# Four projections of a retention branch, each cut into seven block products, with tokens on the partitions

## The chip, the cores and the metric

One core of one Trainium2 chip runs the whole kernel. The metric is the device time of one execution in microseconds (us). The kernel before takes 1122.37 us, the median of three runs that lie between 1118.46 and 1122.79 us. The five engines are named as in the profile: PE (matrix products), DVE (element by element), ACT (scale, copy and functions), POOL and SP (here used almost only to issue DMA transfers). Each engine works through its own queue in order; an instruction that waits holds back everything behind it on that engine.

## What is computed

A decoder layer of width 1024 on 512 tokens. A retention branch with four heads and a latent attention branch read the same normalised input; each is projected to width 1024 and gated; their sum goes through `w_o`, and an MLP and a per-layer embedding follow. The change is in the third line here and the first product of the fourth:

```
ro = retention(q, k, v)                       # 512 tokens x 4 heads x 512
ro = rms_norm(ro, ret_norm)                   # per head: a factor per token, a gain per channel
a_ret = (ro * silu(rg)) @ w_br                # the branch: (512 x 2048) @ (2048 x 1024)
mixed = sigmoid(gr) * a_ret + sigmoid(gm) * a_mla
x = x + mixed @ w_o
```

Per head the branch is a product of 512 tokens x 512 channels with a 512 x 1024 part of `w_br`, and the four heads are summed.

## The kernel before

**Products.** Everything is float32 in accuracy, made from float32r products: each operand is split into a high part and a low remainder, and `mm3` issues three matmuls (low by high, high by low, high by high), the low part of its stationary operand first. A weight chunk of 512 KB arrives as a 128 x 1024 buffer `wr_...`; ACT copies its high part to `wh_...` (L261) and DVE subtracts to get `wl_...` (L265, or L267 with a sign). Activations are split in the same way by `split` (ACT L306, DVE L307).

**Steps.** The program is a list of steps, each with the key of its weight chunk. `run_steps` goes through it: the split of a chunk is put one step ahead of the step that uses it, its transfer three steps ahead; there are three split buffers and six raw ones. PE's order is that of the list. The other engines follow the order in which the scheduler placed their instructions.

**Block products.** Some projections (`rv`, `rg`, `up`/`dn`) are done as a set of seven block products (numbered 1 to 7) in place of eight: some of their weights are a sum of two blocks, and this sum is made in the transfer. For product 7 POOL issues a second transfer that adds a block onto the buffer already loaded by SP, for 5 another; the weights of 6 and 4 are added onto the buffer of 7 after its previous value was split. So 5 transfers on SP and 4 adding ones on POOL serve one chunk set.

**A retention head.** Steps `rq` (2), `rk` (2), for heads 0 and 2 fourteen steps `rv` that serve two heads, seven steps `rg` with scores (`rs`), the weighted sum (`ro`) and the statistics between them. DVE reads `rq` and `rk` out of PSUM for the rotation (L774, L775: two products per block; L780, L781: the combination) and splits them. The gated output `og` has channels on partitions.

**The branch of a head** runs during the next head: `ret_factor` multiplies `og` by the factor per token, which PE first spreads over the partitions (`pbo`, four small transposes), and splits it to `rog`; `branch_r` then is four steps of 24 matmuls, with the weights stationary and 512 tokens on the free dimension, each giving two of the eight 128-channel blocks of the sum. ACT copies a result out (`rt`), and POOL adds it onto a buffer in memory, one of eight per head (head 0 writes). For heads 1 and 3 the four branch steps follow `rk`; for head 2 they stand between the first `rv` steps. Behind head 3 the sum comes back (`re`), the last head's branch adds its result from PSUM with DVE (L867), `mix` applies the two gates' results (L897, L898) and splits for `wo`.

## Time and profile before

| | us |
|---|---|
| median of three runs | 1122.37 |
| the profiled execution | 1125.78 |
| its span | 1124.0 |
| PE busy, share of the span | 1107.5, 99% |
| DVE busy, share | 734.9, 65% |
| ACT busy, share | 536.7, 48% |
| head 1 begins (first `rq` matmul) | 374.7 |
| head 2 begins | 451.4 |
| head 3 begins | 570.7 |
| tail begins (`gr` step 5) | 647.4 |
| the run of `wo` products begins | 689.2 |
| first `up` product | 730.3 |

The profiled execution is 3.4 us above the median of the runs, and 1.8 us of it lie outside the span. The granted clock of PE was 0.997 of full speed on average. The page of a profile gives sums per engine, the chain of work that ended last, and the costliest groups; a timeline gives one engine's instructions with the idle time before each and what ended it.

### The profile page before, as it was taken

Reading aid. Unit: us, or ns where it says so; the run is one execution under the profiler, and the core shown is the slowest. Engines: PE = TensorE matmul, PEld = TensorE weight load, DVE = VectorE, ACT = ScalarE, POOL = GpSimd, SP = SyncE. Lnnn points to the kernel's source line nnn. Section 1 sums busy time; section 2 is a strip of 40 time slices with the busy share of each in tenths; the row PEclk is TensorE's granted clock in tenths of the full one; section 3 lists DMA queues with packets and bytes.
Section 4 is the critical chain, followed back from the end, with each engine's and each line's share of the span. In section 5 each row is a group of like instructions: output and inputs, shape, how many; then the busy total and the mean of one; then the engine's idle time right before and its main releaser. Section 6 shows DMA issues by size and latency. Waiting matters only on the chain.

```text
span 1124.0 us, 14722 instructions
## 1 busy us (share of the span) xinstructions
PE 1107.5 (99%) x5549; PEld 939.0 (84%) x5549; DVE 734.9 (65%) x1206; ACT 536.7 (48%) x762; POOL 85.4 (8%) x113
## 2 busy tenths in 40 slices
...
GB/s 264 59 98 106 67 99 57 128 210 211 190 225 173 87 212 121 135 202 253 137 92 220 223 172 154 196 274 117 171 165 168 176 166 155 186 123 219 146 29 75
DMA packets 59223, 175.97 MB, mean 157 GB/s; under 512 B 7248, under 2 KB 8656, under 8 KB 58896
## 3 DMA queue, kind: packets, MB, share of 16 engines
q1 hardware_dynamic: 45168, 129.66, 33.8%
q0 software_dynamic: 13840, 45.36, 20.9%
...
q10 hardware_dynamic: 144, 0.03, 0.0%
...
## 4 chain that ended last, share of the span: by engine, by line
PE 87%; DVE 4%; DMA 4%; ACT 2%; issue 2%; SPq 0%; ACTq 0%; DVEq 0%; POOLq 0%
PE up L168 16%; PE dn L168 14%; PE br L168 6%; PE rg L168 5%; PE rv L168 5%; PE pg L168 4%; PE gr L168 4%; PE rq L168 4%; PE rk L168 4%; PE bm L168 4%; PE wo L168 4%; DMA wr_rg<-wstream 4%; PE gm L168 3%; PE ro L168 3%; PE sc L168 2%
## 5 line engine op out<-in xcount | busy, mean ns | idle before, releaser
L168 PE MATMUL dn<-wh_dn,cl 128*128 128x512 f32 x224 | 87.2, 389 | 0.0
L168 PE MATMUL dn<-wh_dn,ch 128*128 128x512 f32 x224 | 87.2, 389 | 0.0
L168 PE MATMUL dn<-wl_dn,ch 128*128 128x512 f32 x224 | 87.1, 389 | 0.0
L261 ACT ACTIVATE wh_dn<-wr_dn 128x1024 fp32r<-128x1024 f32 x32 | 34.0, 1062 | 75.5 <-PE up L168 54.3
L261 ACT ACTIVATE wh_up<-wr_up 128x1024 fp32r<-128x1024 f32 x32 | 33.9, 1061 | 57.4 <-PE up L168 29.3
L265 DVE TENSOR_TENSOR wl_dn<-wr_dn,wh_dn 128x1024 fp32r<-128x1024 f32 x32 | 39.0, 1220 | 27.5 <-ACT wh_dn L261 27.5
L265 DVE TENSOR_TENSOR wl_rg<-wr_rg,wh_rg 128x1024 fp32r<-128x1024 f32 x20 | 24.3, 1223 | 40.7 <-ACT wh_rg L261 40.4
L265 DVE TENSOR_TENSOR wl_up<-wr_up,wh_up 128x1024 fp32r<-128x1024 f32 x32 | 39.1, 1222 | 17.4 <-ACT wh_up L261 17.4
L970 DVE SCALAR_TENSOR_TENSOR f<-up,bcx 128x512 f32<-128x512 f32 x32 | 20.6, 685 | 44.1 <-PE up L168 44.1
L168 PEld LDWEIGHTS dn<-wl_dn,ch 128*128 128x128 f32 x224 | 42.0, 188 | 8.8
L168 PEld LDWEIGHTS dn<-wh_dn,cl 128*128 128x128 f32 x224 | 42.0, 188 | 8.7
L168 PEld LDWEIGHTS dn<-wh_dn,ch 128*128 128x128 f32 x224 | 42.0, 188 | 8.6
L261 ACT ACTIVATE wh_dn<-dr_dn 128x1024 fp32r<-128x1024 f32 x24 | 25.5, 1060 | 42.2 <-PE up L168 29.1
L223 POOL DMA_DIRECT2D dr_dn<-wstream x24 | 21.4, 892 | 306.3 <-DMA dr_dn<-wstream 182.0
L265 DVE TENSOR_TENSOR wl_dn<-dr_dn,wh_dn 128x1024 fp32r<-128x1024 f32 x24 | 29.3, 1222 | 22.4 <-ACT wh_dn L261 22.4
L261 ACT ACTIVATE wh_rv<-wr_rv 128x1024 fp32r<-128x1024 f32 x28 | 29.6, 1058 | 28.7 <-PE rv L168 11.8
L261 ACT ACTIVATE wh_rg<-wr_rg 128x1024 fp32r<-128x1024 f32 x28 | 29.3, 1054 | 28.9 <-DMA wr_rg<-wstream 23.6
L265 DVE TENSOR_TENSOR wl_br<-wr_br,wh_br 128x1024 fp32r<-128x1024 f32 x16 | 19.5, 1219 | 21.6 <-ACT wh_br L261 21.6
L1028 DVE TENSOR_TENSOR d<-d,dn 128x1024 f32<-128x1024 f32 x24 | 29.2, 1219 | 6.5 <-PE dn L168 6.5
L265 DVE TENSOR_TENSOR wl_rv<-wr_rv,wh_rv 128x1024 fp32r<-128x1024 f32 x20 | 24.4, 1223 | 13.6 <-ACT wh_rv L261 13.6
L861 ACT ACTIVATE rt<-br 128x512 f32<-128x512 f32 x24 | 14.3, 596 | 36.1 <-PE br L168 30.9
L644 ACT ACTIVATE p<-p,ng,hr 128x128 f32<-128x128 f32 (+3 forms) x32 | 20.6, 646 | 15.6 <-DVE ng L642 15.5
...
## 6 DMA issues: line engine op xcount, KB each, us to landing
...
```

Of the source, the lines that this page charges most:

```text
L168: return tc.keep_in_program_order(nc.tensor.matmul(*a, **k))
L223: nc.gpsimd.dma_start(raw, chunk(("w", blk, kb, fb, c)), accum_op=ALU.add)
L261: i = ACT(hi, raw, AF.Copy, scale=sign)
L265: TT(lo, raw, hi.bitcast(F32), op=ALU.subtract)
L644: ACT(cols[b], cols[b], AF.Exp, bias=ng[:, b:b + 1], scale=d["rq"][:, b], accum_out=sums[:, b:b + 1])
L861: ACT(t, ps, AF.Copy)
L970: STT(u[:, i], ps[:, i], 0.0, V["bcx2"], op0=ALU.max, op1=ALU.mult)
L1028: TT(to, to, dps[p], op=ALU.add if sign > 0 else ALU.subtract)
```

## The change

The branch of each head becomes a set of seven block products, each 12 matmuls. Its stationary operand is now the gated output (256 channels by 256 tokens, two blocks of 128 channels), its moving one a 256 x 512 weight block held as 128 x 1024, so tokens lie on the partitions of the result. The operands are blocks of `og` or a sum or difference of two, kept in `bs` and `bt`, and split to `bx` (head, product, h or l). The factor of a token is now a scalar per partition: ACT applies it (with its sign, `ro` or `nro`) when it reads the result (`rt`), or DVE for the last head. Two results per product are added onto memory, fourteen per head. `ret_factor`, `pbo` and `rog` are gone. The steps are laid between the next head's `rq` and `rk`. In the tail the sum comes back with tokens on partitions, DVE adds the last head's fourteen results, 32 transposes on PE (`ret_turn`) turn it, and `mix` reads PSUM. The weights come as for the other block products.

```diff
--- before.py
+++ after.py
@@ -52,7 +52,7 @@
 
 C_ID, C_MASK, C_IND, C_INVR, C_INVM, C_SGN, C_N = 0, 128, 256, 260, 261, 262, 263
 
-NDYN, NKEEP, NW, NRAW, NDRAW, AHEAD, PREP, EARLY, PAD = 45, 16, 3, 6, 4, 1, 3, 5, 104
+NDYN, NKEEP, NW, NRAW, NDRAW, AHEAD, PREP, EARLY, PAD = 47, 16, 3, 6, 4, 1, 3, 5, 72
 GROUPS = DFF // 1024
 
 
@@ -105,8 +105,6 @@
         for key, o in (("rq", O_RQ), ("rk", O_RK)):
             for n in range(2):
                 add((key, h, n), "w_in", full, _rng(o + h * RQK + n * P, P))
-        for k in range(4):
-            add(("br", h, k), "w_br", _rng(h * RV, RV), _rng(2 * k * P, 2 * P))
 
     for kb in range(2):
         for fb in range(2):
@@ -114,6 +112,7 @@
                 for c in range(2):
                     add(("w", ("rv", q), kb, fb, c), "w_in", _rng(kb * S + c * 2 * P, 2 * P), _rng(O_RV + (2 * q + fb) * RV, RV))
             for h in range(RH):
+                add(("w", ("br", h), kb, fb, 0), "w_br", _rng(h * RV + kb * 256, 256), _rng(fb * S, S))
                 add(("w", ("rg", h), kb, fb, 0), "w_in", _rng(kb * S, S), _rng(O_RG + h * RV + fb * 256, 256))
     for gg in range(GROUPS):
         for n in range(8):
...
@@ -797,14 +796,14 @@
 
     def ret_attend(h):
         d = R[h]
+        d["o"] = [dyn.tile([P, 2, S], F32, tag="o2", name=f"og{h}{k}", bufs=2) for k in range(2)]
         for m in range(4):
             ps = B(f"ro{h}{m}")
             for j in range(4):
                 N = max(256, (4 - j) * P)
                 mm3(ps[:, S - N:S], cut(d["v"][j], m * P), at(j), j == 0, j == 3)
-            t, sq = T(f"og{h}{m}"), T(f"sqo{h}{m}")
-            ACT(t, ps, AF.Copy, scale=g(G_RET + 4 * h + m))
-            d["og"].append(t)
+            sq = T(f"sqo{h}{m}")
+            ACT(d["o"][m // 2][:, m % 2], ps, AF.Copy, scale=g(G_RET + 4 * h + m))
             ACT(sq, ps, AF.Square)
             if m:
                 TT(d["sq"], d["sq"], sq, op=ALU.add)
...
@@ -837,40 +838,83 @@
                 d["z"][12] = T(f"z{h}_12")
             TT(d["z"][blk], z, sg, op=ALU.mult)
 
+    def two(t):
+        return t.rearrange("p (k c) -> p k c", k=2)
+
     def ret_gated(h):
         d = R[h]
-        for m in range(4):
+        for k in range(2):
             for r in range(2):
-                cs, z = slice(r * 256, r * 256 + 256), d["z"][10 * (r + 1) + 1 + m // 2]
-                TT(d["og"][m][:, cs], d["og"][m][:, cs], z[:, m % 2 * 256:m % 2 * 256 + 256], op=ALU.mult)
-
-    def ret_factor(h):
-        d, r = R[h], R[h]["r"]
-        bc = bcast(B(f"pbo{h}"), lambda b: r[:, b:b + 1])
-        for m in range(4):
-            TT(d["og"][m], d["og"][m], bc, op=ALU.mult)
-            new = K if m < 2 and h < RH - 1 else T
-            d["rog"][m] = split(d["og"][m], None, hi=new(f"rog{h}{m}h", F32R), lo=new(f"rog{h}{m}l", F32R))
-
-    def branch_r(w, h, half):
+                o = d["o"][k][:, :, r * 256:r * 256 + 256]
+                TT(o, o, two(d["z"][10 * (r + 1) + 1 + k]), op=ALU.mult)
+
+    def branch_operand(h, p):
+
+        (a, b), lo_, hi_ = R[h]["o"], slice(0, 256), slice(256, 512)
+        if p == 7:
+            R[h]["s"] = T(f"bs{h}")
+        sv = two(R[h]["s"]) if "s" in R[h] else None
+        if p in (1, 2, 4):
+            src = (a if p == 1 else b)[:, :, hi_ if p == 4 else lo_]
+        elif p == 5:
+            src = two(T(f"bt{h}"))
+            TT(src, a[:, :, hi_], b[:, :, hi_], op=ALU.subtract)
+        else:
+            src = sv
+            if p == 7:
+                TT(sv, a[:, :, hi_], a[:, :, lo_], op=ALU.subtract)
+            else:
+                TT(sv, b[:, :, hi_ if p == 6 else lo_], sv, op=ALU.subtract)
+        hi, lo = two(T(f"bx{h}{p}h", F32R)), two(T(f"bx{h}{p}l", F32R))
+        split(src, None, hi=hi, lo=lo)
+        R[h]["x", p] = [(hi[:, k], lo[:, k]) for k in range(2)]
+
+    brps = {}
+
+    def branch_r(w, h, p):
+
+        ch, d = CHAIN[p], R[h]
+        if p in (1, 7, 2):
+            brps[ch] = [B(f"br{h}{p}{i}") for i in range(2)]
+        for k in range(2):
+            for i in range(2):
+                mm3(brps[ch][i], cut(d["x", p][k], i * P), cut(w, k * S, S), p in (1, 7, 2) and k == 0, k == 1,
+                    skip_group_check=True)
+        to, f = {1: (11, "nr"), 7: (22, "r"), 6: (21, "nr"), 2: (11, "r"), 5: (22, "r"), 4: (21, "nr"), 3: (12, "r")}[p]
         for i in range(2):
-            n = 2 * half + i
-            ps = proj(B(f"br{h}{n}"), R[h]["rog"], w, i * P, 2 * P)
-            if h < RH - 1:
-                t = T(f"rt{h}{n}")
-                ACT(t, ps, AF.Copy)
-                if h == 0:
-                    ret[n] = aside(f"ret{n}", t)
-                else:
-                    nc.gpsimd.dma_start(ret[n], t, accum_op=ALU.add)
+            b, n = 2 * (to // 10 - 1) + i, to % 10 - 1
+            r, ps = d[f][:, b:b + 1], brps[ch][i]
+            if h == RH - 1:
+                STT(ret[b, n], ps, r, ret[b, n], op0=ALU.mult, op1=ALU.add)
+                continue
+            t = T(f"rt{h}{p}{i}")
+            ACT(t, ps, AF.Copy, scale=r)
+            if h == 0 and p in (1, 7, 6, 3):
+                ret[b, n] = aside(f"ret{b}{n}", t)
             else:
-                TT(ret[n], ret[n], ps, op=ALU.add)
+                nc.gpsimd.dma_start(ret[b, n], t, accum_op=ALU.add)
+
+    def ret_back():
+        for b in range(4):
+            for n in range(2):
+                t = K(f"re{b}{n}")
+                nc.sync.dma_start(t, ret[b, n])
+                ret[b, n] = t
+
+    trp = {}
+
+    def ret_turn(n):
+
+        trp[n] = B(f"tr{n}")
+        for b in range(4):
+            MM(trp[n][:, b * P:b * P + P], ret[b, n // 4][:, n % 4 * P:n % 4 * P + P], ident, is_transpose=True,
+               start=b == 0, stop=b == 3, skip_group_check=True)
 
...
     def mix(n):
         if n < EARLY:
             ACT(sgr[n], sgr[n], AF.Sigmoid)
-        TT(ret[n], ret[n], sgr[n], op=ALU.mult)
-        TT(ret[n], ret[n], zm[n], op=ALU.add)
-        mixed[n] = split(ret[n], f"mix{n}")
+        TT(sgr[n], trp[n], sgr[n], op=ALU.mult)
+        TT(sgr[n], sgr[n], zm[n], op=ALU.add)
+        mixed[n] = split(sgr[n], f"mix{n}")
 
 
...
+    def branch_steps(h, seq):
+
+        order = [p for p in seq if not callable(p)]
+        step(None, branch_operand, h, order[0])
+        for p in seq:
+            if callable(p):
+                p()
+                continue
+            if order.index(p) < 6:
+                step(None, branch_operand, h, order[order.index(p) + 1])
+            step(("sw", ("br", h), p, 0), branch_r, h, p)
+
     for h in range(RH):
-        for key in ("rq", "rk"):
-            for n in range(2):
-                step((key, h, n), ret_qk, h, key, n)
-                if h and (key, n) == ("rq", 0):
-                    step(None, ret_factor, h - 1)
-        left = [(("br", h - 1, k), branch_r, h - 1, k) for k in range(4 if h else 0)]
+        def qk(key, n, h=h):
+            return lambda: step((key, h, n), ret_qk, h, key, n)
+
+        qk("rq", 0)()
+        if h:
+            branch_steps(h - 1, [1, qk("rq", 1), 7, 2, qk("rk", 0), 6, 5, qk("rk", 1), 4, 3])
+        else:
+            for key, n in (("rq", 1), ("rk", 0), ("rk", 1)):
+                qk(key, n)()
         for p in (1, 7, 2, 6, 5, 4, 3) if h % 2 == 0 else ():
             for c in range(2):
                 step(("sw", ("rv", h // 2), p, c), ret_v, h // 2, p, c)
             if h == 0 and p in (1, 7, 2):
                 step(None, x_operand, {1: 6, 7: 5, 2: 3}[p])
-            if left:
-                step(*left.pop(0))
-        for st in left:
-            step(*st)
         for p in (1, 7):
             step(("sw", ("rg", h), p, 0), ret_gate, h, p)
         step(None, ret_scores, h)
@@ -1219,17 +1274,19 @@
         for p in (4, 3):
             step(("sw", ("rg", h), p, 0), ret_gate, h, p)
         step(None, ret_gated, h)
+    step(None, ret_back)
     for n in range(8):
         step(None, reload, n)
-    for n in range(EARLY, 8):
-        step(("gr", n), gate_r, n)
-        if n == EARLY:
-            step(None, ret_factor, RH - 1)
-    for k in range(4):
-        step(("br", RH - 1, k), branch_r, RH - 1, k)
-        step(None, mix, 2 * k)
-        step(None, mix, 2 * k + 1)
-    for n in range(2):
+    step(("gr", 5), gate_r, 5)
+    branch_steps(RH - 1, [1, 7, 2, lambda: step(("gr", 6), gate_r, 6), 6, 5, 4, 3])
+    for n in range(4):
+        step(None, ret_turn, n)
+        step(None, mix, n)
+    step(("gr", 7), gate_r, 7)
+    for n in range(4, 8):
+        step(None, ret_turn, n)
+        step(None, mix, n)
+    for n in range(3):
         step(("o", n), out_part, n, 0)
     for n in range(8):
         step(("o", n), out_proj, n)
```

The order of the instructions, as built, at three places. In the names, `br070` is head 0, product 7, chunk 0; `bx01` is head 0, product 1; the last number tells a buffer apart. Line numbers of the kernel after are its own.

DVE, from the first reads of head 1's `rq` (L774, L775). Before:

```order
L774 TENSOR_TENSOR rqa10_3906<-rq10_3881,trc_952 128x512
L775 TENSOR_TENSOR rqb10_3907<-rq10_3881,trs_953 128x512
L851 TENSOR_TENSOR og00_3691<-og00_3691,pbo0_3910 128x512
L851 TENSOR_TENSOR og01_3708<-og01_3708,pbo0_3910 128x512
L851 TENSOR_TENSOR og02_3726<-og02_3726,pbo0_3910 128x512
L307 TENSOR_TENSOR rog00l_3917<-og00_3691,rog00h_3916 128x512
L851 TENSOR_TENSOR og03_3744<-og03_3744,pbo0_3910 128x512
L307 TENSOR_TENSOR rog01l_3922<-og01_3708,rog01h_3921 128x512
L307 TENSOR_TENSOR rog02l_3927<-og02_3726,rog02h_3926 128x512
L265 TENSOR_TENSOR wl_rk_1_1_3983<-wr_rk_1_1_3980,wh_rk_1_1_3982 128x1024
L307 TENSOR_TENSOR rog03l_3932<-og03_3744,rog03h_3931 128x512
```

And now (L773, L774 are the same reads):

```order
L773 TENSOR_TENSOR rqa10_3902<-rq10_3877,trc_952 128x512
L774 TENSOR_TENSOR rqb10_3903<-rq10_3877,trs_953 128x512
L264 TENSOR_TENSOR wl_br070_3950<-wr_br070_3922,wh_br070_3949 128x1024
L306 TENSOR_TENSOR bx01l_3907<-og00_3678,bx01h_3906 128x512
L865 TENSOR_TENSOR bs0_3910<-og00_3678 128x512
L306 TENSOR_TENSOR bx07l_3913<-bs0_3910,bx07h_3912 128x512
L867 TENSOR_TENSOR bs0_3910<-og01_3679,bs0_3910 128x512
L264 TENSOR_TENSOR wl_br020_3997<-wr_br020_3925,wh_br020_3996 128x1024
L773 TENSOR_TENSOR rqa11_3978<-rq11_3953,trs_953 128x512
L774 TENSOR_TENSOR rqb11_3979<-rq11_3953,trc_952 128x512
L779 TENSOR_TENSOR rqa10_3902<-rqa10_3902,rqa11_3978 128x512
L780 TENSOR_TENSOR rqb10_3903<-rqb10_3903,rqb11_3979 128x512
```

Where the scaled `og` was split for a branch three PE steps later, the weights and operands of products 1 and 7 now stand between the reads of the two `rq` blocks; the matmuls of product 1 stand between those two blocks on PE.

DVE again, from there on to the operand of product 2, which PE needs two steps behind the second `rq`:

```order
L779 TENSOR_TENSOR rqa10_3902<-rqa10_3902,rqa11_3978 128x512
L780 TENSOR_TENSOR rqb10_3903<-rqb10_3903,rqb11_3979 128x512
L264 TENSOR_TENSOR wl_rk_1_0_4030<-wr_rk_1_0_4027,wh_rk_1_0_4029 128x1024
L306 TENSOR_TENSOR rqx1l_3985<-rqa10_3902,rqx1h_3984 128x512
L264 TENSOR_TENSOR wl_br060_4058<-wr_br070_3922,wh_br060_4057 128x1024
L306 TENSOR_TENSOR rqy1l_3989<-rqb10_3903,rqy1h_3988 128x512
L306 TENSOR_TENSOR bx02l_3993<-og01_3679,bx02h_3992 128x512
```

The low part of product 2's operand stands behind the combination of `rq` and two splits of weights.

DVE in the tail, ahead of the second `wo` weight. Before:

```order
L897 TENSOR_TENSOR re4_6366<-re4_6366,ge4_6370 128x512
L897 TENSOR_TENSOR re5_6372<-re5_6372,gr5_6415 128x512
L898 TENSOR_TENSOR re4_6366<-re4_6366,ze4_6368 128x512
L898 TENSOR_TENSOR re5_6372<-re5_6372,ze5_6374 128x512
L867 TENSOR_TENSOR re6_6376<-re6_6376,br36_6657 128x512
L307 TENSOR_TENSOR mix4l_6642<-re4_6366,mix4h_6641 128x512
L897 TENSOR_TENSOR re6_6376<-re6_6376,gr6_6473 128x512
L307 TENSOR_TENSOR mix5l_6648<-re5_6372,mix5h_6647 128x512
L867 TENSOR_TENSOR re7_6380<-re7_6380,br37_6671 128x512
L898 TENSOR_TENSOR re6_6376<-re6_6376,ze6_6378 128x512
L897 TENSOR_TENSOR re7_6380<-re7_6380,gr7_6506 128x512
L265 TENSOR_TENSOR wl_o_1_6700<-wr_o_1_6697,wh_o_1_6699 128x1024
```

And now:

```order
L941 TENSOR_TENSOR gr5_6497<-tr5_6800,gr5_6497 128x512
L306 TENSOR_TENSOR mix3l_6752<-ge3_6454,mix3h_6751 128x512
L942 TENSOR_TENSOR ge4_6458<-ge4_6458,ze4_6456 128x512
L942 TENSOR_TENSOR gr5_6497<-gr5_6497,ze5_6460 128x512
L941 TENSOR_TENSOR gr6_6614<-tr6_6811,gr6_6614 128x512
L306 TENSOR_TENSOR mix4l_6797<-ge4_6458,mix4h_6796 128x512
L942 TENSOR_TENSOR gr6_6614<-gr6_6614,ze6_6462 128x512
L306 TENSOR_TENSOR mix5l_6808<-gr5_6497,mix5h_6807 128x512
L941 TENSOR_TENSOR gr7_6786<-tr7_6822,gr7_6786 128x512
L306 TENSOR_TENSOR mix6l_6819<-gr6_6614,mix6h_6818 128x512
L942 TENSOR_TENSOR gr7_6786<-gr7_6786,ze7_6464 128x512
L264 TENSOR_TENSOR wl_o_1_6836<-wr_o_1_6833,wh_o_1_6835 128x1024
```

In both orders nearly all of the mix stands ahead of this weight. Before, its combinations follow the last head's additions from PSUM (L867), one per block; now they read turned blocks (L941), which PE turns after the additions of the last head (L888).

## The prediction

> **What bounds the kernel now.** I read the page's engines first, then the chain of work that ended last.

> ```profile
> span 1124.0 us, 14722 instructions
> PE 1107.5 (99%) x5549; PEld 939.0 (84%) x5549; DVE 734.9 (65%) x1206; ACT 536.7 (48%) x762; POOL 85.4 (8%) x113
> PE 87%; DVE 4%; DMA 4%; ACT 2%; issue 2%; SPq 0%; ACTq 0%; DVEq 0%; POOLq 0%
> ```

> PE is busy nearly all the time, and 87% of the chain is PE. So two things can change the end: how much work PE has, and how often it stands. The stretches which the change touches, by windows (columns: length, then busy time of PE, weight loads, DVE, ACT, POOL, then granted clock, DMA share, GB/s), and the pieces of the chain in them (start, length, what):

> ```profile
> 374.70:397.00 22.30, 22.30 (x102) 18.45 (x101) 18.02 (x33) 8.37 (x11) 0.86 (x1) 1.00 0.42 120
> 397.00:418.70 21.70, 21.70 (x98) 17.96 (x98) 8.50 (x10) 9.25 (x13) 5.61 (x9) 1.00 0.68 212
> 664.20:689.20 25.00, 24.45 (x109) 19.90 (x108) 22.56 (x34) 10.15 (x13) 0.00 (x0) 1.00 0.35 115
> ```
> ```profile
> 374.71 5.47 PE rq L168 x24
> 380.18 0.44 PE pbo L168 x4
> 380.62 5.48 PE rq L168 x24
> 386.09 10.88 PE rk L168 x48
> 396.97 21.76 PE br L168 x96
> 418.73 5.75 PE rg L168 x48
> ...
> 647.36 5.46 PE gr L168 x24
> ...
> 689.20 41.09 PE wo L168 x180
> ...
> 1060.83 1.75 PE tr L168 x16
> ```

> Head 1's `rq`, `rk` and the branch of head 0 take 418.73 - 374.71 = 44.02 us without a gap. DVE is 81% busy (18.02 of 22.30) in the first half, beside `rq` and `rk`, and 39% in the second, beside `br`. In the tail it is 90% busy. The 65% of the page hides this: where the new work is put, DVE has little room, and what counts is the place in its queue.

> **The change on PE.** A `br` matmul takes 21.76 / 96 = 0.2267 us. Per head 4 x 24 = 96 become 7 x 12 = 84, so 48 fewer in all: -10.9 us. The four `pbo` go: 4 x 0.44 = -1.8. Thirty-two transposes come; 16 such take 1.75, so +3.5. Net -9.1 us of PE work. If PE stays full, that is the gain.

> **The change on DVE and ACT, heads 1 to 3.** Their prices, from the timelines of these engines (start, duration, what; in brackets the idle time before and what ended it):

> ```profile
> 380.22 0.69 DVE L774 TENSOR_TENSOR rqa<-rq,trc 128x512 f32<-128x512 f32 x1 [1.79 <-PE rq L168]
> 380.82 0.68 DVE L775 TENSOR_TENSOR rqb<-rq,trs 128x512 f32<-128x512 f32 x1
> ...
> 389.75 1.21 DVE L265 TENSOR_TENSOR wl_br<-wr_br,wh_br 128x1024 fp32r<-128x1024 f32 x1
> 390.89 0.68 DVE L307 TENSOR_TENSOR rqx1l<-rqa,rqx1h 128x512 fp32r<-128x512 f32 x1
> 391.49 0.68 DVE L307 TENSOR_TENSOR rqy1l<-rqb,rqy1h 128x512 fp32r<-128x512 f32 x1
> ...
> 666.93 0.69 DVE L867 TENSOR_TENSOR re<-re,br 128x512 f32<-128x512 f32 x1
> ```
> ```profile
> 380.26 1.06 ACT L261 ACTIVATE wh_rk<-wr_rk 128x1024 fp32r<-128x1024 f32 x1 [3.97 <-issue]
> ...
> 400.13 0.58 ACT L861 ACTIVATE rt<-br 128x512 f32<-128x512 f32 x1
> ...
> 652.86 0.60 ACT L888 ACTIVATE gr<-gr 128x512 f32<-128x512 f32 x1 [1.44 <-PE gr L168]
> ```

> From start to start, a 128x512 operation holds DVE for 0.60 us (380.22 to 380.82) and a weight split for 1.14 (389.75 to 390.89); a result is there after 0.68. DVE reads `rq` 0.04 us after PE's end (380.18), ACT starts 0.08 after. A split of the weights on ACT takes 1.06, a read of PSUM there about 0.60. The new reading with a factor and the addition in one instruction (L888 of the kernel after) do not occur before; the nearest rows are the 0.58 of `rt` and the 0.69 of L867. Bounds: as these rows, or half as much again; I take the rows.

> The total of DVE work matters less than the order listed above. The first matmul of a product needs the low part of its operand, and that stands on DVE behind work that waits for PE itself. I count from the first matmul of `rq0` of a head, now with the previous head's branch:

> - `rq0` ends at 5.47. Then DVE does two reads (to 6.71), the weight split of product 7 (ACT's half waits for the end of `rq0` too, since of the three split buffers it takes the one of `rq0`; 5.55 + 1.06 = 6.61, in time), to 7.85, and `bx01l`, ready at 8.53. PE stands **3.1 us**, where product 1 should have begun.
> - Product 1 ends at 11.3 (12 x 0.2267 = 2.72), `rq1` at 16.7, product 7 at 19.5. Product 2 needs `bx02l`: behind the end of `rq1` four operations (2.40), a weight split (1.14), `rqx1l` (0.60), another weight split (1.14), `rqy1l` (0.60) and itself (0.68): 6.56 after 16.8, so 23.3. PE stands **3.9 us**.
> - Product 2 ends at 26.1, `rk0` at 31.5, product 6 at 34.2. Product 5 adds in PSUM where 6 was, so it waits until ACT has read it, and ACT's queue has the weight split of product 4 first, which waits for the end of 6: 1.06 + 0.60. PE stands **1.7 us**.
> - Product 5 ends at 38.6, `rk1` at 44.1, product 4 at 46.8. Product 3 needs `bx03l` behind the four operations on `rk1` and two weight splits, as product 2 did: 44.1 + 6.56 = 50.7. PE stands **3.9 us**, and the piece ends at 53.4.

> Check: work 21.9 (the four `rq`, `rk`) + 19.0 = 40.9, stalls 12.6, in all 53.4 or 53.5. Against 44.02 that is +9.4 per head, for three heads **+28.2 us**. The 12.6 us are fourfold what the head saves on PE (44.0 - 40.9 = 3.1). If all DVE rows were free behind the reads, product 1 would still lose about 2; if the weights of a step ran late too, another microsecond or two: 6 to 12 per head.

> For head 2 the branch no longer stands between the `rv` steps. That stretch lost 2.6 us of idle PE time before its `ro`, more than head 0's 1.6 (clock rows below): between 0 and -2.6, I take **-1**.

> **The tail**, from the start of `gr` step 5. That ends at 5.46; ACT does its sigmoid (row at 652.86) ahead of `bx31h`, then DVE `bx31l`, so product 1 begins at 7.4, 1.9 late. 7, 2, `gr` 6 and 6 follow until 23.7. The operand of product 5 stands on DVE behind the low weight part of product 4, whose adding transfer cannot start before the weights of 6 are split, and that split stands behind the last head's additions of product 2: 15.6 + 1.2 + 1.14 = 17.9. The nearest transfers are the ones for `rg`, with the queues' shares:

> ```profile
> 350.57 5.51 DMA wr_rg<-wstream
> ...
> 533.43 8.62 DMA wr_rg<-wstream
> ```
> ```profile
> q1 hardware_dynamic: 45168, 129.66, 33.8%
> q0 software_dynamic: 13840, 45.36, 20.9%
> ...
> ret0d<-rt POOLq DMA_DIRECT2D x3, 256.0 KB, 7.4
> ```

> So the weights land at 23.7 to 26.8, and after ACT (1.06), DVE (1.14) and the operand (0.68) product 5 begins at 26.6 to 29.7, 2.9 to 6.0 late. From there DVE is never idle: behind that weight, before the second `wo` weight is split, come 11 operations of the branch, 23 of the mix (34 x 0.60 = 20.4) and four weight splits (4.6), 25.0 in all. `wo`'s second product begins at 50.9 to 54.0; before, it began at 689.20 - 647.36 = 41.8. So +9.1 to +12.2, middle **+10.6**; the removed `rog` work has been left out here, as it stood ahead of this chain.

> **The clock.** One stall in the trace before was followed by slow PE, another was not:

> ```profile
> 355.90:358.90 3.00, 1.40 (x9) 1.00 (x7) 1.62 (x3) 2.71 (x5) 0.00 (x0) 1.00 0.20 81
> ...
> 548.00:551.00 3.00, 2.42 (x17) 2.08 (x15) 1.92 (x5) 0.52 (x2) 0.00 (x0) 1.00 0.91 269
> 551.00:554.00 3.00, 1.03 (x4) 0.83 (x5) 2.17 (x4) 2.96 (x5) 0.00 (x0) 0.91 0.04 5
> 554.00:557.00 3.00, 3.00 (x12) 2.71 (x11) 1.55 (x2) 1.17 (x2) 0.00 (x0) 0.52 0.73 243
> ```
> ```profile
> 358.89 6.29 PE ro L168 x38
> ...
> 553.36 7.84 PE ro L168 x38
> ```

> 1.6 us idle of 3 left the clock at 1.00; 2.0 of 3 (2.6 with the slice before) brought 0.52 for the next 3 us, and the same 38 matmuls took 7.84 in place of 6.29: 1.55 us lost. The new stalls of over 2.8 us are three per head and two in the tail (product 5 and `wo`), 11 in all: between 0 and 11 x 1.55 = 17.1. By the two rows most are long enough; I take 8 of 11, **+12.4**.

> [...]

> **Sum.** 28.2 - 1 + 10.6 + 12.4 = +50.2 us. The trace's execution took 1125.78, 3.4 above the median of 1122.37; so the runs should give 1122.4 + 50.2 = 1172.6, about **1173 us**, slower. With the bounds: 28.2 - 2.6 + 9.1 = 34.7 gives 1157, 28.2 + 12.2 + 17.1 = 57.5 gives 1180.

> **Rivals.**
> - *The stalls come, the clock stays full*: no 12.4, so 1160. For it: the row at 355.90; against it, that at 554.00.
> - *Transfers become the bound.* From q1's row 512 KB cost 0.338 x 1124 / 129.66 x 0.524 = 1.5 us of all DMA engines, from q0's 2.7 (half for a 256 KB result). A head adds one load, four adding transfers and six results: 1.5 + 10.9 + 8.2 = 20.6, on 0.42 x 22.3 + 0.68 x 21.7 = 24.1 used now. That is 45 of 53.4 us, 84%, so not the bound on average. But products 6 and 4 wait for adding transfers; if each came 3.1 us late (8.62 - 5.51) in three heads, 18.6 more: 1191.
> - *Part of the stalls is covered*, because I put DVE waits in a row that in truth overlap: half of 37.8 and little clock loss, 1140 to 1150.
> - *PE stays full, the kernel is faster*: 1122.4 - 9.1 = 1113. It is one mechanism, operands split in time, and decides once the four stalls of a head are below 3.1 us together. For it speaks that DVE has idle time beside `br` (61%); against it, that the operand stands in DVE's queue behind reads of the `rq` that PE computes directly before. I see no row that moves it forward.

> **Chances.** Forecast 0.58 (its own range 1164 to 1181), clock full 0.20, transfers 0.10, part covered 0.07, PE full 0.03, an even balance between saved work and stalls 0.02. What can be told from no change is 0.5%, about 5.6 us. The range from 1150 to 1190 leaves out PE full, the balance, the lower part of "part covered" and the far end of the transfers. Faster 0.03, same 0.03, slower 0.94.

> **What would show it.** In the profile after, each head's first product should begin about 8.5 us after its `rq0`, with DVE `bx01l` as the releaser; products 2 and 3 about 23 and 51 us after, released by `bx02l` and `bx03l`; product 5 by ACT's reading. From `rq0` to the first `rg` should be 53 us and more, by the clock. In the tail the waits should be for `bx35l` and for `wl_o`. PE's busy share should fall, and the row of granted clock should dip there. I am wrong if PE's stalls sum to under 3 us per head, if they stand before `wh` of the branch's weights waiting for DMA, or if the heads take 44 us and the time went elsewhere.

## The result and the profile after

The changed kernel takes **1200.23 us** (median of four runs, 1195.78 to 1201.62) against 1122.58 us for the kernel before: a ratio of 1.0694, 95% interval 1.0657 to 1.0732. It is slower, as predicted, but by 78 us where 50 were predicted, and the time lies 10 us above the predicted range. The profiled execution has a span of 1199.0 us against 1124.0, so 75.0 us are to be found in the traces.

The page of the changed kernel, its engines and the granted clock in 40 slices:

```profile
span 1199.0 us, 14811 instructions
...
PE 1125.3 (94%) x5517; PEld 945.9 (79%) x5517; DVE 763.5 (64%) x1224; ACT 567.9 (47%) x804; POOL 115.7 (10%) x147
...
PEclk9999999999999889899999998899999999999999
```

PE has 32 instructions fewer (5517 in place of 5549) and yet is busy for 17.8 us longer. The mean granted clock is 0.974 in place of 0.997, and the dips of the clock row lie in the first two of the three pieces with a branch and in the tail (the third has 0.92 in the window view below).

The waits of PE in the branch of head 0, from PE's timeline (start, duration, what; in brackets the idle time before it and what ended it), then the longest one of head 2, the three of the tail, and one behind it:

```profile
387.43 0.79 PE L167 MATMUL br<-wh_br,bx01l 128*128 128x512 f32 x1 [3.12 <-DVE bx01l L306]
405.39 0.76 PE L167 MATMUL br<-wh_br,bx02l 128*128 128x512 f32 x1 [4.03 <-DVE bx02l L306]
420.62 0.50 PE L167 MATMUL br<-wh_br,bx05l 128*128 128x512 f32 x1 [1.72 <-ACT rt L891]
435.74 0.79 PE L167 MATMUL br<-wh_br,bx03l 128*128 128x512 f32 x1 [3.94 <-DVE bx03l L306]
...
663.34 0.80 PE L167 MATMUL br<-wh_br,bx23l 128*128 128x512 f32 x1 [5.44 <-DVE bx23l L306]
...
708.92 0.50 PE L167 MATMUL br<-wh_br,bx31l 128*128 128x512 f32 x1 [3.08 <-DVE bx31l L306]
729.65 0.77 PE L167 MATMUL br<-wh_br,bx35l 128*128 128x512 f32 x1 [3.86 <-DVE re L888]
756.71 0.77 PE L167 MATMUL wo<-mix0h,wl_o 128*128 128x512 f32 x1 [4.60 <-DVE wl_o L264]
...
803.38 0.80 PE L167 MATMUL up<-x2g0h,wl_up 128*128 128x512 f32 x1 [3.18 <-DVE xr L966]
```

The four waits of head 0 are 3.12, 4.03, 1.72 and 3.94 us; 3.1, 3.9, 1.7 and 3.9 had been counted out of the order of the queues. The window view of the three heads' pieces (from the first `rq` of a head to its first `rg`), of the tail up to `wo`'s second product, and of `wo` up to the first `up` (length, busy time of PE, weight loads, DVE, ACT and POOL, granted clock, DMA share, GB/s):

```profile
378.69:441.03 62.34, 49.53 (x183) 38.93 (x181) 32.84 (x49) 26.20 (x36) 13.77 (x19) 0.84 0.73 179
473.69:533.06 59.37, 46.51 (x183) 36.70 (x182) 32.83 (x49) 26.26 (x36) 14.65 (x17) 0.92 0.82 183
606.95:667.58 60.63, 46.32 (x182) 36.74 (x181) 32.93 (x49) 26.11 (x36) 15.63 (x18) 0.92 0.85 190
700.21:756.71 56.50, 44.95 (x203) 36.30 (x201) 44.91 (x70) 24.98 (x35) 1.73 (x2) 0.93 0.48 150
756.71:803.38 46.67, 43.49 (x180) 35.44 (x180) 25.41 (x31) 16.91 (x23) 0.00 (x0) 0.94 0.54 175
```

Where the 75.0 us are, from the starts of the stages in the two traces:

| stage | before | after | difference |
|---|---|---|---|
| up to the first `rq` of head 0 | 279.50 | 283.80 | +4.3 |
| the three pieces with a branch | 3 x 44.02 worth of the same work | 62.34, 59.37, 60.63 | +50.3 |
| the rest of the heads | | | -1.7 |
| tail, `gr` step 5 to `wo`'s second product | 41.84 | 56.50 | +14.7 |
| from there to the first `up` | 41.09 | 46.67 | +5.6 |
| to the end | 393.71 | 395.62 | +1.9 |

(For head 2 the branch stood between the `rv` steps before; what it gained there is in "the rest". Some starts of before are those of the chain, 0.16 us behind the timeline's; by timelines alone no row would change by more than 0.2.)

```profile
383.06:386.47 3.41, 1.26 (x6) 0.71 (x4) 2.12 (x3) 1.58 (x2) 0.00 (x0) 1.00 0.84 239
386.47:389.89 3.42, 2.46 (x6) 1.98 (x7) 2.69 (x5) 0.63 (x1) 0.86 (x1) 0.50 0.46 68
389.89:393.30 3.41, 3.41 (x10) 2.64 (x9) 0.20 (x1) 1.04 (x2) 0.58 (x1) 0.50 0.50 95
417.19:420.61 3.42, 1.71 (x8) 1.09 (x6) 3.24 (x5) 2.40 (x5) 0.00 (x0) 1.00 0.29 89
478.63:482.05 3.42, 0.69 (x4) 0.22 (x2) 2.70 (x4) 1.58 (x2) 0.00 (x0) 1.00 0.79 235
482.05:485.46 3.41, 3.03 (x7) 2.45 (x8) 2.31 (x4) 0.63 (x1) 0.85 (x1) 0.50 0.47 79
485.46:488.87 3.41, 3.41 (x16) 2.81 (x16) 0.33 (x1) 2.32 (x3) 1.69 (x2) 1.00 0.61 84
724.39:727.80 3.41, 1.40 (x7) 0.82 (x5) 0.79 (x1) 1.87 (x3) 0.00 (x0) 1.00 0.44 159
727.80:731.21 3.41, 1.56 (x4) 1.32 (x5) 3.41 (x6) 1.69 (x3) 0.00 (x0) 0.50 0.44 151
731.21:734.63 3.42, 3.42 (x10) 2.68 (x9) 1.44 (x2) 0.00 (x0) 0.00 (x0) 0.50 0.43 146
```

PE idles 2.15 us of the window from 383.06, and the next is granted half the clock. The wait runs on into that one: 0.96 us of it are idle too, and the one after it is slow as well. At 417.19 only 1.71 us are idle, and the clock stays full. At 478.63 it is 2.72 us, but the slow window that follows is idle for only 0.38 us, and the clock comes back at once. So the same wait of 3.12 us costs 2.9 us of clock in head 0 (half of 2.46 and of 3.41) and 1.5 us in head 1 (half of 3.03); the two differ in where the wait lay on the grid. In the whole trace there are 13 such spells behind the start, which cost 26.0 us by this sum (half of PE's busy time in each slow window); in the trace before there is one, 1.7 us. All eleven stalls that the prediction had priced with a clock loss are among the 13. One more stall is as long and has no slow window behind it: the 3.08 us before the tail's first product. The grid cuts it in two, and the two windows of full clock are idle for 1.49 and 1.59 us.

### The profile page after: what moved, and what is told of

It is laid out like the page before. It is cut to its first block, busy times and chain, and to the rows that moved or that the text cites. A ratio compares the mean times of both kernels' runs of the same rounds, so it can differ in the third digit from the quotient of the medians.

```text
span 1199.0 us, 14811 instructions
## 1 busy us (share of the span) xinstructions
PE 1125.3 (94%) x5517; PEld 945.9 (79%) x5517; DVE 763.5 (64%) x1224; ACT 567.9 (47%) x804; POOL 115.7 (10%) x147
## 5 line engine op out<-in xcount | busy, mean ns | idle before, releaser
L260 ACT ACTIVATE wh_up<-wr_up 128x1024 fp32r<-128x1024 f32 x32 | 34.0, 1062 | 53.4 <-PE up L167 29.3
L264 DVE TENSOR_TENSOR wl_up<-wr_up,wh_up 128x1024 fp32r<-128x1024 f32 x32 | 39.1, 1223 | 20.6 <-ACT wh_up L260 20.6
L1014 DVE SCALAR_TENSOR_TENSOR f<-up,bcx 128x512 f32<-128x512 f32 x32 | 20.6, 686 | 44.2 <-PE up L167 44.2
L264 DVE TENSOR_TENSOR wl_br<-wr_br,wh_br 128x1024 fp32r<-128x1024 f32 x20 | 24.4, 1223 | 36.0 <-ACT wh_br L260 36.0
L260 ACT ACTIVATE wh_rg<-wr_rg 128x1024 fp32r<-128x1024 f32 x28 | 29.4, 1056 | 34.1 <-DMA wr_rg<-wstream 17.9
L260 ACT ACTIVATE wh_br<-wr_br 128x1024 fp32r<-128x1024 f32 x28 | 29.5, 1055 | 25.7 <-issue 16.3
L891 ACT ACTIVATE rt<-br,ro 128x512 f32<-128x512 f32 x24 | 16.0, 686 | 31.1 <-PE br L167 28.4
```

What stands on the lines that cost most here:

```text
L260: i = ACT(hi, raw, AF.Copy, scale=sign)
L264: TT(lo, raw, hi.bitcast(F32), op=ALU.subtract)
L891: ACT(t, ps, AF.Copy, scale=r)
L1014: STT(u[:, i], ps[:, i], 0.0, V["bcx2"], op0=ALU.max, op1=ALU.mult)
```

## The experiments

The first question was whether the rest of the loss is the clock. My theory A is what was said above: the stalls as predicted, with a clock loss nearly twice the size taken (22.8 us behind the eleven stalls, where 12.4 had been taken). The rivals were the transfers, and VectorE in the tail. The prediction had also not foreseen +4.3 us ahead of the heads and the wait before `up`. Kernel names in the headings are those of the runs.

### e1_fill: PE is kept busy in the waits

```diff
+        pad = {1: 13, 2: 17, 3: 17}.get(p, 0) if h < RH - 1 else {5: 16}.get(p, 0)
+        for j in range(pad):
+            MM(brps["a" if p == 1 else "b"][0], xn[j % 8][0][:, 0:P], xn[7][0], start=True, stop=True, skip_group_check=True)
...
+            for j in range(19 if n == 1 else 0):
+                MM(wo_ps[n], mixed[j % 4][0][:, 0:P], mixed[3][0], start=True, stop=True, skip_group_check=True)
```

> The kernel after, with extra matmuls on operands that are long there, put on PE exactly where it stands: 13 before product 1 (2.9 us), 17 before products 2 and 3 (3.9 us each) of the three heads, 16 before product 5 of the last head (3.6) and 19 before the second wo product (4.3). Their results are overwritten. They neither shorten a wait nor take work away; they only keep PE from being idle. Theory A (the idle time itself halves the clock, and this costs some 20 us over the three heads and 5 in the tail beside the stalls): no slow spell in the heads, each head's piece from rq0 to rg 53.5 to 55 us in place of 62.3, 59.4 and 60.6, the whole about 1176, 24 less than 1200, although 250 matmuls were added. Rival B (PE is slow after a wait for another reason, such as the load on the DMA or the operands): the same slow spells, 1200. Rival C (the extra matmuls delay what follows): up to 1210.

Measured: **1179.93 us**, ratio 1.0513 (1.0487 to 1.0538). With 176 more matmuls (13 + 17 + 17 in three heads, 16 and 19 in the tail; the 250 of the expectation was a miscount) the kernel is 20.3 us faster. PE's timeline shows that the operand comes as late as before, 8.75 us after the head's first `rq` matmul at 377.48 (8.74 in the changed kernel):

```profile
386.23 0.50 PE L167 MATMUL br<-wh_br,bx01l 128*128 128x512 f32 x1 [0.17 <-DVE bx01l L306]
```

Head 1's piece, from its first `rq` to its first `rg` at 432.19, takes 54.71 us in place of 62.34, near the 53.4 of the prediction without any clock loss; the second takes 54.77. The third takes 59.19, more than the 53.5 to 55 expected: its wait for `bx23l` was longer than the fill, 3.06 us of it are left, and a slow stretch follows (from 652.33 on its matmuls start 0.43 us apart, from 655.38 on 0.23). The slow windows left in this trace cost 5.0 us by the same sum, 21.0 less than after; its span is 21.0 us shorter. So the clock's part is shown, with its size; rivals B and C are refuted.

### e2_lead2: each operand of the heads is made one product earlier

```diff
-            if order.index(p) < 6:
-                step(None, branch_operand, h, order[order.index(p) + 1])
+            if order.index(p) + lead < 7:
+                step(None, branch_operand, h, order[order.index(p) + lead])
...
-            branch_steps(h - 1, [1, qk("rq", 1), 7, 2, qk("rk", 0), 6, 5, qk("rk", 1), 4, 3])
+            branch_steps(h - 1, [1, qk("rq", 1), 7, 2, qk("rk", 0), 6, 5, qk("rk", 1), 4, 3], 2, qk("rq", 0))
```

> The kernel after, with each branch operand of the three heads split one product earlier: products 1 and 7 ahead of rq0's reads, product 2 ahead of rq1's, product 3 ahead of rk1's. The amount of work is the same. Theory A (the place of the operand in DVE's queue makes the stalls of 3.1, 4.0 and 3.9 us): these three go in each head and with them the slow spells; left is the wait of product 5 for the reading of product 6, about 1 to 1.7 us. Each head's piece takes 42 to 43 us in place of 62.3, 59.4 and 60.6; in all 53 to 56 us less, about 1145. Rival B (weights or transfers are the next limit: adding transfers for products 6 and 4, results on their way out of the buffers): stalls of 2 us and more remain, before the weights or the operand of product 6, 4 or 5; 1155 to 1180. Rival C (DVE's amount of work is the bound, not its order): little change, 1190 and more.

Measured: **1173.12 us**, ratio 1.0438 (1.0406 to 1.0470); theory A had said about 1145, and the time is in the range of rival B. The waits for `bx01`, `bx02` and `bx03` are gone in all three heads, so DVE's queue was their cause. But the pieces take 47.62, 42.16 and 51.80 us where 41 would be PE's work. ACT's timeline of this kernel, and the window in which it waits the longest:

```profile
409.37 1.31 ACT L891 ACTIVATE rt<-br,nro 128x512 f32<-128x512 f32 x2 [3.97 <-DMA ret21d<-rt]
...
523.66 1.06 ACT L260 ACTIVATE wh_rv<-wr_rv 128x1024 fp32r<-128x1024 f32 x1 [10.46 <-DMA wr_rv<-wstream]
...
621.59 0.69 ACT L891 ACTIVATE rt<-br,nro 128x512 f32<-128x512 f32 x1 [6.22 <-DMA ret21d<-rt]
```
```profile
501.52:525.00 23.48, 16.72 (x74) 13.56 (x72) 5.89 (x7) 8.66 (x12) 7.01 (x8) 0.94 1.08 251
```

ACT can't read a result, because its buffer `rt` is still being sent; PE then waits 3.61 us (head 0) and 8.05 us (head 2) before product 5. `rv`'s weights come late too, in a stretch in which the DMA share is at its full (1.08; a packet counts whole where it starts, so a short window can pass 1). My reading is that with the stalls the same transfers had longer pieces to fit into, and that without them they are the next bound: the prediction's rival of the transfers, reached in full only when the stalls are gone. The next two runs ask this.

### e5_pair and e7_eight: fewer transfers of results

Of fourteen results per head, two and two belong to the same block. e5_pair is e2_lead2, with the two added by DVE first, so that eight are sent:

```diff
+            if p in (1, 7, 6):
+                R[h]["t", b, n] = t
+            elif p == 3:
+                out(h, b, n, t)
             else:
-                nc.gpsimd.dma_start(ret[b, n], t, accum_op=ALU.add)
+                late.append((h, b, n, t))
...
+        while late:
+            hh, b, n, t = late.pop(0)
+            u = R[hh]["t", b, n]
+            TT(u, u, t, op=ALU.add)
+            out(hh, b, n, u)
```

> The kernel with earlier operands (1173 us), where two results for the same block are first added to each other in the core's memory (six additions of 0.60 us on DVE per head, each put one product later), so that a head sends eight results as before the change, not fourteen. Theory A (with the operands in time the transfers are the next limit: product 5 waited 3.6, 1.1 and 8.1 us because a buffer for its reading was still on its way out, and rv waited 6.8 us for weights): product 5 waits 1 to 1.7 us in each head, the head pieces 42 to 43.5 us in place of 47.6, 42.2 and 51.8, the wait in rv under 2 us; 1148 to 1155. Rival B (DVE's added work brings the stalls of the operands back): pieces of 46 us and more with a wait for a bx operand; 1165 to 1180. Rival C (the adding transfers of the weights, which stay, are the limit): waits before products 6 and 4 for wh_br; 1160 to 1170.

e7_eight is e2_lead2 with six of the fourteen results not sent and nothing added:

```diff
-            else:
+            elif p in (1, 7, 6, 3):
                 nc.gpsimd.dma_start(ret[b, n], t, accum_op=ALU.add)
```

> The kernel with earlier operands (1173 us), where the second results of a block (products 2, 5 and 4 of the three heads) are read from PSUM as before but not sent, so that their part is missing from the sum: eight result transfers per head, and no added work on DVE. Theory A (the number of result transfers makes the waits that are left): as in the pairing run, 1148 to 1155, or 1 to 3 us less than it. Rival C (the weights' adding transfers, not the results): within 5 us of 1173.

Measured: **1154.22 us** (ratio 1.0275, 1.0246 to 1.0304) and **1158.09 us** (1.0302, 1.0268 to 1.0337). Six transfers per head are worth 15 to 19 us, whether their additions are made elsewhere or not at all. e7_eight had been expected no slower than e5_pair, and it is 3.9 us slower, with a wait of 4.20 us before `rv` in place of 2.18; why stays open. The heads' pieces of e5_pair by windows:

```profile
379.66:422.52 42.86, 41.14 (x182) 33.71 (x181) 34.06 (x52) 25.25 (x35) 6.42 (x9) 1.00 0.75 194
455.15:496.00 40.85, 40.75 (x181) 33.28 (x180) 33.55 (x52) 24.83 (x34) 7.74 (x9) 1.00 0.77 183
573.50:616.50 43.00, 41.28 (x184) 33.84 (x183) 32.46 (x50) 23.79 (x32) 7.49 (x9) 1.00 0.79 188
```

The clock is full in all three. These are 40.9 us of work and at most one wait of 1.72 us, the one before product 5, and the heads gain about 1 to 3 us each on the 44.02 of before. What the change saves on PE does arrive here. The loss that is left, 31 us against the kernel before, lies elsewhere: from `gr` step 5 to the first `up` this kernel takes 102.9 us, the kernel before 82.9.

### e3_before_qp and e4_bank: the two parts that were not foreseen

The change took the `qp` buffers out of a pool of their own (six) and put them into the common one, by two lines that read like bookkeeping. e3_before_qp is the kernel before with these two lines alone:

```diff
-NDYN, NKEEP, NW, NRAW, NDRAW, AHEAD, PREP, EARLY, PAD = 45, 16, 3, 6, 4, 1, 3, 5, 104
+NDYN, NKEEP, NW, NRAW, NDRAW, AHEAD, PREP, EARLY, PAD = 47, 16, 3, 6, 4, 1, 3, 5, 104
...
-            t = dyn.tile([P, S], F32R, tag="qp", name=f"qp{gq}{i}", bufs=6)
+            t = dyn.tile([P, S], F32R, tag="t", name=f"qp{gq}{i}")
```

> The kernel before, with one thing of the change: the eight small qp tiles of the attention's rotary part come from the common pool of 47 buffers and have no six buffers of their own. Theory A (this alone made the attention part 4.3 us longer: an operand's buffer is free only when the transfer out of it has landed, a stall of 2.3 us with a slow spell behind it, and another of 1.4): rq0 of head 0 begins near 283.8 in place of 279.5, the whole 1126 to 1128. Rival B (the 4.3 us came from another part of the change, or from the order of a single execution): 1122, and 279.5.

Measured: **1127.92 us**, ratio 1.0041 (1.0016 to 1.0065), beside 1122.63 for the kernel before: +5.3 us, by the interval 1.8 to 7.3. The timelines of ACT and PE in this run, the same place of the changed kernel, and ACT's of the kernel before:

```profile
159.13 0.47 ACT L309 ACTIVATE v21h<-pv,f 128x256 fp32r<-128x256 f32 x1 [3.17 <-DMA qp<-qr11h]
...
163.21 1.74 PE L168 MATMUL pbk<-cst,hr 128*128 128x128 f32 x8 [2.24 <-DVE hr L605]
```
```profile
159.81 0.48 ACT L308 ACTIVATE v21h<-pv,f 128x256 fp32r<-128x256 f32 x1 [3.16 <-DMA qp<-qr11h]
...
163.89 0.84 PE L167 MATMUL pbk<-cst,hr 128*128 128x128 f32 x6 [2.27 <-DVE hr L604]
```
```profile
158.34 0.47 ACT L309 ACTIVATE v21h<-pv,f 128x256 fp32r<-128x256 f32 x1
```

`v21h` now takes a buffer of the common pool that the transfer into `qp` still reads. ACT waits 3.2 us, DVE behind it, PE 2.2 us, and a slow stretch follows (the matmuls `sc` of 256 columns start 0.21 us apart from 164.96, 0.11 from 166.87). Head 0's `rq` then begins 3.7 us later than before, where the changed kernel loses 4.3. So these two lines account for most of the loss ahead of the heads. The rest of what this execution lost (its span is 6.4 us longer) lies behind that, first of all in a wait of 2.84 us before head 0's `ro`. The changed kernel's trace doesn't have it and that of e4_bank does (2.71), so whether the two lines bring it stays open.

e4_bank is the changed kernel with one small transpose more ahead of the last `wo` product, which takes a PSUM bank and so shifts the rotation by one:

```diff
+    def skip():
+        MM(B("skip")[:, 0:P], ident, ident, is_transpose=True, start=True, stop=True)
+
...
+        if n == 7:
+            step(None, skip)
```

> The kernel after, with one small transpose (0.1 us) into a PSUM buffer of its own ahead of the last wo product, so that this product's bank is not one of the two that the first up product takes. Theory A (the first up product stands 3.2 us because it takes the bank of the last wo product, which DVE must first read; before it took that of the one before): the stall is gone, with the 1.5 us of slow clock behind it; about 1195.5, 4.7 less. Rival B (up waits for the x2 operands anyway): the stall only changes its name, 1199 to 1200.

Measured: **1196.05 us**, ratio 1.0648 (1.0617 to 1.0679), 4.2 us less than the changed kernel. The two intervals overlap, so the time alone doesn't decide; the trace does. From `wo`'s second product to the end it takes 438.8 us in place of 442.3, 3.5 less where 4.7 were expected; the other 2.1 of the difference in span lie ahead of the tail, where the two programs are the same. What remains at this place on PE's timeline are the two short waits for the last operand:

```profile
803.31 0.51 PE L167 MATMUL up<-x2g7h,wl_up 128*128 128x512 f32 x1 [0.21 <-ACT x2g7h L308]
804.09 0.51 PE L167 MATMUL up<-x2g7l,wh_up 128*128 128x512 f32 x1 [0.28 <-DVE x2g7l L311]
```

The change alters the number of banks taken ahead of `wo`, and by that the first `up` product got the bank of the last `wo` product, which DVE had yet to read (`xr` L966 in the row at 803.38).

### e6_all and e8_best: all remedies at once

e6_all is e5_pair with the order of a head's products drawn apart further, the tail's operands ahead of `gr`, the first `wo` product between the last turned blocks, half of the `qp` buffers elsewhere, and the PSUM bank of `up` free. Its core:

```diff
-            branch_steps(h - 1, [1, qk("rq", 1), 7, 2, qk("rk", 0), 6, 5, qk("rk", 1), 4, 3], 2, qk("rq", 0))
+            branch_steps(h - 1, [-1, -7, q0, -2, 1, -6, q1, 7, -5, k0, 2, -4, 6, -3, k1, 5, 4, 3])
...
-    step(("gr", 5), gate_r, 5)
-    branch_steps(RH - 1, [1, 7, 2, lambda: step(("gr", 6), gate_r, 6), 6, 5, 4, 3])
+    branch_steps(RH - 1, [-1, -7, gr(5), -2, 1, -6, 7, 2, -5, 6, gr(6), -4, 5, -3, 4, 3])
```

A negative number is the making of that product's operand. (The expectation speaks of two `wo` products between the turned blocks; the edit moves one.)

> Pairing and earlier operands, and beside them: product 2 behind rk0 and products 5, 4, 3 behind rk1 (so that no product stands right behind the one whose result it adds to), the operand of product 3 ahead of rk1; in the tail the first operands ahead of gr step 5, product 6 ahead of gr step 6 (its split lets the transfer for product 4 start earlier), and the first two wo products between the last turned blocks, so that their weights are split earlier; half of the qp tiles in the two buffers that og uses later; no bank of the last wo product for the first up product. Theory A (these are all of the causes): early part as before (279.5 to rq0), head pieces 41 to 42.5 us against 44.0 of before, tail from gr 5 to the second wo product 42 to 46 us against 41.8, up without a stall: 1117 to 1126, about as before the change. Rival B (DVE's amount of work in the tail is the bound: some 43 us of it from gr 5 on): tail 48 us and more, 1126 to 1135. Rival C (transfers in the heads remain the bound): head pieces of 45 us and more, 1130 to 1150.

Measured: **1137.53 us**, ratio 1.0140 (1.0108 to 1.0172); its profiled execution lies 8 us above that. The time is above A and B, in the range of C alone, but what B and C name both shows in the trace: the heads' pieces take 44.51, 40.82 and 44.72 us, and from `gr` step 5 to the first `up` it is 92.4 us against 82.9 before. It is better than any run so far, and still slower than before. Left in its trace are, among others, 5.32 us of PE ahead of `rv`, 3.12 ahead of the tail's first product. e8_best goes on from there:

```diff
+        elif h == 2:
+            branch_steps(h - 1, [-1, -7, q0, -2, 1, q1, -6, 7, k0, 2, -5, k1, rv[0], 6, rv[1], -4, 5, rv[2], -3, 4, rv[3], 3] + rv[4:])
+        else:
+            branch_steps(h - 1, [-1, -7, q0, -6, 1, -2, q1, 7, -5, k0, 6, 2, -4, 5, -3, k1, 4, 3])
...
+        if h == RH - 1:
+            tc.keep_in_program_order(ACT(hi, src, AF.Copy))
```

> All of the changed kernel's parts, as in e6_all, with three further shifts: the order of a head's products keeps an operand one product ahead and a result one product behind throughout; in the head with rv, the last block products lie between steps of rv, so that the transfers of the sum have rv's 22 us of products as cover; in the last head, ScalarE's copies of the product operands stand ahead of the sigmoid of the reloaded gate, which waits for its DMA. Theory A (what was left in e6_all was the wait for a result's buffer in head 3, 1.8 to 2.0 us, for rv's wts, 5.3, for ro, 2.3, and the tail's first operand, 3.1): these 12 us and a window of clock or two go, 1119 to 1127. Rival B (the number of transfers of a head sets a floor: they only come out elsewhere): 1130 to 1138, with the wait at another row of the same transfers. Rival C (the tail is bound by VectorE): heads at 41 us each, but the tail's piece stays over 50 us, 1126 to 1131.

Measured: **1137.76 us** (1130.46 to 1144.11), ratio 1.0115 (1.0071 to 1.0158). No gain over e6_all: this is what rival B had said, though the kernel was built to reach A. The six runs lie in two groups, 1130 to 1133 and 1142 to 1144, and the trace is of the upper one. The wait for the tail's first operand is gone, but others stand on PE's timeline:

```profile
516.08 0.50 PE L167 MATMUL rv<-wh_rv,s50l 128*128 128x512 f32 x1 [3.90 <-ACT cv L746]
556.13 0.38 PE L167 MATMUL ro<-ath,rv1211l 128*128 128x256 f32 x1 [3.07 <-ACT ath L305]
617.56 0.80 PE L167 MATMUL br<-wh_br,bx23l 128*128 128x512 f32 x1 [4.67 <-DVE bx23l L306]
```

The engines named stand there because of a transfer. On ACT's timeline the copy of `rv`'s weights waits for its load, and `cv` is next in the queue; the copy of `bx23` waits for a buffer of the common pool that a result's transfer still reads:

```profile
514.49 1.06 ACT L260 ACTIVATE wh_rv<-wr_rv 128x1024 fp32r<-128x1024 f32 x1 [4.26 <-DMA wr_rv<-wstream]
...
614.12 0.63 ACT L305 ACTIVATE bx23h<-bs 128x512 fp32r<-128x512 f32 x1 [7.13 <-DMA ret00d<-rt]
```

### e9_noadd and e10_nosend: which transfers are left

Both start from e8_best. e9_noadd omits the sixteen adding transfers of the branch's weights, e10_nosend the sixteen of the results of heads 1 and 2:

```diff
+                if blk[0] == "br":
+                    return chunk(("w", blk, kb, fb, c))
                 nc.gpsimd.dma_start(raw, chunk(("w", blk, kb, fb, c)), accum_op=ALU.add)
```

> e8_best without the 16 adding transfers of the branch's weights (4 per head): the products take the quarters as they lie, so the branch's part of the result is another, and the time is read as that of the same products with 16 transfers fewer. In e8_best the transfers are busy 97% of the stretch in which rv waits 3.9 us (501 to 535 us), and head 3's product 3 waits 4.7 us. Theory A (the transfers of the branch are what is left of the loss): both waits and the slow clock behind them go, 10 to 14 us less, 1123 to 1128. Rival B (the places in the queues of VectorE and ScalarE): the waits stay where they are, 1134 to 1140.

```diff
-        else:
+        elif h == 3:
             nc.gpsimd.dma_start(ret[b, n], t, accum_op=ALU.add)
```

> e8_best without the 16 adding transfers of the results of heads 1 and 2 (they are computed and added in pairs, but not sent, so their part of the sum is missing). Theory A (transfers): a result's transfer is half as large as one of the weights, but they are the ones right ahead of rv's weights; 6 to 12 us less, 1126 to 1132, with rv's wait under 1.5 us. Rival B (the queues of VectorE and ScalarE): as e8_best, 1134 to 1140.

Measured: e9_noadd **1136.64 us** (ratio 1.0115, 1.0079 to 1.0151), e10_nosend **1128.42 us** (1.0042, 1.0018 to 1.0065). So theory A falls for the weights: the ratio is that of e8_best, and the 10 to 14 us expected lie outside the noise (some 6 us by the two intervals). Their removal shortens head 3's wait for `bx23` from 4.67 to 0.23 us, but `rv` still waits 3.77 and `ro` 2.97. It holds for the results: the ratio is 0.0073 lower, about 8 us (3 to 14 by the two intervals), no run of e10_nosend is as slow as the fastest of e9_noadd, and both waits are gone. The stretch of `rv` of e8_best, 501.14 to 535.16 us, by windows, and the issues in the transfer view from 485 to 530 us (what, queue, count, KB each, median us from issue to landing), first of e8_best:

```profile
501.14:535.16 34.02, 29.47 (x121) 23.45 (x120) 18.17 (x23) 16.03 (x21) 6.12 (x7) 0.95 0.97 249
```
```profile
wr_rv<-wstream POOLq DMA_DIRECT2D x6, 512.0 KB, 11.0
wr_rv<-wstream SPq DMA_DIRECT2D x5, 512.0 KB, 8.8
...
ret20d<-rt POOLq DMA_DIRECT2D x1, 256.0 KB, 13.7
```

and the same window of e10_nosend, whose `rv` ends at 530.74:

```profile
501.14:535.16 34.02, 34.01 (x167) 28.50 (x167) 23.28 (x26) 19.93 (x26) 5.13 (x6) 1.00 0.99 268
```
```profile
wr_rv<-wstream SPq DMA_DIRECT2D x6, 512.0 KB, 4.9
wr_rv<-wstream POOLq DMA_DIRECT2D x6, 512.0 KB, 7.6
```

The transfers are as busy without the results (0.99) as with them (0.97), but PE has no wait. So the share of the transfers alone does not tell whether they bind. The last results of head 1 (`ret20d` among them) are sent just as `rv`'s weights are wanted, and these land after 8.8 and 11.0 us in place of 4.9 and 7.6. That it is the order of the transfers, and not their number, is not shown: no run kept the number and changed the order. The time that POOL takes to issue them is not the reason alone, for e9_noadd takes away as many issues.

What is left in e10_nosend lies behind the heads. The tail, from `gr` step 5 to the first `up`, by windows, of the kernel before and of e10_nosend:

```profile
647.36:730.29 82.93, 82.38 (x365) 67.88 (x365) 57.95 (x86) 33.73 (x46) 0.00 (x0) 1.00 0.55 175
```
```profile
637.68:729.44 91.76, 87.29 (x382) 70.49 (x381) 68.62 (x98) 40.49 (x56) 1.71 (x2) 0.96 0.55 175
```

Head 3 ends 9.7 us earlier than before (637.68 against 647.36), which is about what the seven products save in three heads. The tail then takes 8.8 us longer: 10.7 us more work on DVE, PE idle for 4.5 us in place of 0.6, a clock of 0.96, and the transposes. The rest of the kernel takes 3.5 us longer in this profile (397.2 against 393.7). A version that keeps the results on the chip and lightens DVE in the tail was not built; no kernel here beats the one before.

## Why the prediction was right and wrong

**The direction and its cause were right.** The operand of a product stands in DVE's queue behind reads of the `rq` or `rk` that PE computes directly before; the four waits of head 0 came within 0.15 us of the count (12.81 us in sum against 12.6). Head 2 waits 14.30, because its last operand came 1.5 us later still: ACT could not write it before a result had been sent out of the buffer that it takes.

```profile
661.29 0.63 ACT L305 ACTIVATE bx23h<-bs 128x512 fp32r<-128x512 f32 x1 [1.73 <-DMA ret21d<-rt]
```

In all that is 39.97 us against 37.8. e2_lead2, which moves these operands alone, takes these waits away.

**The step that failed is the term for the clock**: "I take 8 of 11, +12.4". All eleven named stalls had a slow spell behind them, and together they cost 22.8 us, 2.07 each and not 1.55. Both factors were too low. The price had been read from the one slow spell in the trace of before, 1.55 us for one slow window. In the changed kernel five of the eleven waits left 0.96 to 1.85 us idle in the next window of the grid too; that window and the one after it were slow, and each of the five cost 2.5 to 2.9 us. My upper bound of 11 x 1.55 = 17.1 was therefore not a bound. The two rows at hand (no loss at 1.6 us idle, a loss at 2.6) allowed all eleven; I had no reason to leave three out. (One stall of 3.1 us escaped, the tail's 3.08, which the grid cut into 1.49 and 1.59 us; the three of 3.1 us in the heads all lost the clock.) e1_fill shows the term directly.

**The other 14.4 us**, since the span is 24.8 us longer than the sum made it and the clock term explains 10.4:

- Ahead of the heads, +4.3: not in the prediction at all. I had read the moved `qp` buffers as having no effect, though a shared pool gives each of its buffers a new predecessor. e3_before_qp shows 3.7 of it in its trace.
- Before `up`, a wait of 3.18 and 1.5 of clock: not foreseen. The rotation of the PSUM banks was not followed past the transposes. In e4_bank the wait is gone, and the kernel from `wo` on is 3.5 us shorter.
- The heads' stalls, +2.2, and the tail's first, 3.08 where 1.9 was counted. There the sigmoid ahead of `bx31h` is that of a reloaded gate, and it waits for the reload itself, as ACT's timeline of the changed kernel shows:

```profile
705.59 0.63 ACT L940 ACTIVATE ge<-ge 128x512 f32<-128x512 f32 x1 [3.63 <-DMA ge<-gr0d]
```

These make 4.3 + 4.7 + 2.2 + 1.2 = 12.4; with the clock's 10.4 that is 22.8 of 24.8. The last 2.0 lie in PE's busy time of the three pieces: less half of that in slow windows it is 41.4 to 41.7 us each, where 40.9 had been counted. (The runs lie 27.6 us above the predicted time, 2.8 more than the spans: the profiled execution of before was 3.4 us above its median, that of the changed kernel was not far from its own.)

**The tail's sum** held: `wo`'s second product was to begin 50.9 to 54.0 us after `gr` step 5. It began at 56.50, with 2.5 us of slow clock behind product 5 and 1.2 for the first operand in it; 52.8 without. Product 5 and `wo` were the two waits named. Product 5's weights came from their transfer 25.7 us after `gr` step 5 (23.7 to 26.8 had been counted), and its operand stands behind them:

```profile
725.93 1.06 ACT L260 ACTIVATE wh_br<-wr_br 128x1024 fp32r<-128x1024 f32 x1 [2.22 <-DMA wr_br<-wstream]
...
728.15 0.68 DVE L306 TENSOR_TENSOR bx35l<-bt,bx35h 128x512 fp32r<-128x512 f32 x1
```

But the wait is not ended by `bx35l`, as had been said. Product 5 adds in PSUM where 6 was, and DVE's reading of 6 (L888) stands right behind `bx35l` in its queue: another 0.8 us. **Head 2** gained 1.5 in its `ro` (the spell of before, at 554 us, is gone), where 1 was taken.

**The rivals.** That the clock stays full is refuted by the grid windows, and that part of the stalls is covered by their sum. The transfers, at 73% to 85% of the heads, cost the changed kernel's heads the 1.5 us of `bx23` and not the 18.6 of the rival; they bind as soon as the stalls are gone. So the condition of that rival was a faster PE, and its place the results' buffers, neither of which the prediction had said. That PE stays full fell with the stalls.
